# Steps between the stages of a two-layer decoder trunk: how norm sums, the last inner tile and the compressed keys reach the matrix engine

## The chip, the cores and the metric

The kernel runs on one core of one Trainium2 chip. The core has five engines, each with an instruction queue of its own that it works off in order: TensorE (PE in the profile; its weight loads are listed as PEld), VectorE (DVE), ScalarE (ACT), GpSimd (POOL) and SyncE (SP), which here issues the DMA transfers. The metric is the device time in microseconds (us) of one execution.

## The reference

One sequence of 256 tokens with 1024 channels goes through two layers. Each layer is a half-step SwiGLU FFN (inner width 2816), a mixer, and a second half-step FFN, each behind an RMS norm and added to the residual `h`:

```python
h = h + 0.5 * swiglu_ffn(rmsnorm(h, ffn1_norm[i]), ffn1_w_in[i], ffn1_w_out[i])
hn = rmsnorm(h, mix_norm[i])
if i < N_A_LAYERS:
    h = h + short_conv_mixer(hn, conv_w_in[i], conv_w[i], conv_w_out[i])
else:
    h = h + nsa_mixer(hn, attn_w_q[j], attn_q_norm[j], attn_w_o[j], rel_bias, kv)
h = h + 0.5 * swiglu_ffn(rmsnorm(h, ffn2_norm[i]), ffn2_w_in[i], ffn2_w_out[i])
```

Layer 1 mixes with a gated short convolution, layer 2 with an attention that has a compressed, a selected and a window branch. Between the layers one shared set of keys and values is made. The compressed keys are `rmsnorm(compress(...))`: blocks of 32 positions go through a two-layer perceptron (`gelu(blk @ w1) @ w2`, 64 output channels, 4 groups, 15 blocks), and the result is normed over the 64 channels. Everything is float32.

## The kernel before

**Products.** Activations lie transposed: channels on the 128 partitions, the 256 tokens along the free axis. A float32 operand is split into a high part (rounded to the type fp32r) and a low part (the rest). An activation tile holds both halves beside each other, 512 columns. For each 128x128 block of weights TensorE makes one product of 512 columns with the weight's high part `wh` (L315, L416) and one of 256 columns with its low part `wl` (L318, L418); the two halves in PSUM are added afterwards (`total`, L327 and L328). Plain float32 products are also used in a few places: TensorE runs each of them as two records.

**Weights.** `Stream` (L98) brings weights in pieces of 128x1024 ("units"): SyncE loads them (`ws`), ScalarE casts the high part (`high`, L148) and VectorE subtracts to get the low part (`low`, L165). There are six buffers for each half. `W.pump()` fills all that is free. The code's order is each engine's order: the kernel is written with a manual schedule, and a call to `W.pump()` puts its casts and subtractions into the queues of ScalarE and VectorE exactly there.

**Stages.** The first half of an FFN (`ffn_in`, L361) runs 22 tiles of two units; each tile's result is drained by `total`, multiplied with the norm's row factor `R`, gated (SiLU) and split into a hidden tile `hid` (`act` in the profile, L321 and L322). The second half (`out_proj`, L394) makes eight column tiles of the residual. For the FFNs each has 22 inner tiles: all high products, then all low ones (L416, L418). For the convolution's output product, with eight inner tiles, the first three column tiles are a "head": k = 0 to 6 of all three, and then k = 7 of each. After a column tile `out_evac` (L385) adds to `h` (L387, VectorE), prepares the next stage's operand `xs` (ScalarE L267, VectorE L271) and sums the squares on GpSimd into `sq` (L285, L286), with one unit's `low` and `high` between. `out_proj` ends with `W.pump()`; so does the attention's output product (L1142).

**The norm.** The next stage starts with `h` times the gain, unnormed; `R` is applied when a tile is drained. `Norm.rows` (L288) multiplies `sq` with a matrix of ones (one float32 product, L291), takes the root on ScalarE (L293) and the reciprocal on VectorE (L295). In the second FFN of each layer and in the convolution, this is done within the first tile: inner tiles 0 to 5, then 6, then `mid()` with the row sums, then 7.

**Tables and compressed keys.** `tables` loads the bias vector `rb` and a one-hot matrix, multiplies them (a float32 product with 33 rows, L250) in the first tile of layer 1's second FFN and writes the result to DRAM. The compressed keys are made in the background of layer 2's first FFN: `c_second` (L739, four groups of 16 columns), `kc_norm` on 16 partitions, `kc_trans` with two transposes.

## Time and profile before

| | |
|---|---|
| time, median of 3 runs | 978.57 us (978.12 to 978.57) |
| the profiled execution's own time | 978.35 us |
| its span, first to last instruction | 976.6 us |
| TensorE busy | 969.2 us (99%) |
| VectorE busy | 739.2 us (76%) |
| ScalarE busy | 559.8 us (57%) |
| GpSimd busy | 160.3 us (16%) |
| granted TensorE clock | 1.000 |

A row of the timeline reads: start, length, engine, line, operation, output <- inputs, shapes, count, and in brackets the idle time before it with what ended it. Rows that follow each other are merged. Matmul records overlap: the distance from start to start is what one costs.

### The profile page before, as it was taken

The numbers are of one execution on the slowest core, as the hardware profiler recorded it, in microseconds if no ns is written. First come the engines' busy times: TensorE is split into PE (matmuls) and PEld (weight loads), VectorE is DVE, ScalarE is ACT, GpSimd is POOL, SyncE is SP. The second block draws the span as 40 slices with busy tenths as digits, with TensorE's granted clock in tenths as the row PEclk, the third lists the DMA queues.
The fourth block names the chain that finished last, engine by engine and source line by source line (L and its number), as shares of the span: only waits on it lengthen the run. The fifth ranks groups of instructions, "written<-read, shape, count | busy, mean of one in ns | idle before, by whom it ended". The sixth has DMA issues, their size and how long they took to land. (4 is left out here: it accounts for less than half of the span.)

```text
span 976.6 us, 14680 instructions
## 1 busy us (share of the span) xinstructions
PE 969.2 (99%) x5680; PEld 845.9 (87%) x5680; DVE 739.2 (76%) x1175; ACT 559.8 (57%) x926; POOL 160.3 (16%) x249
## 2 busy tenths in 40 slices
PE   9999999999999999999999999999999999999998
PEld 7888888888888888888888888888887888888888
DVE  6988766668888778767549987866589898878652
ACT  6666553355556566644546677743489666656530
POOL 2000001144460000011111013001237330000000
PEclk9999999999999999999999999999999999999999
DMA  8565554546546775554635565655510356555550
GB/s 300 199 211 197 178 211 173 179 167 209 187 144 248 225 230 191 178 210 173 215 130 173 173 221 210 216 173 183 212 46 1 133 191 219 192 179 206 182 189 22
DMA packets 28289, 177.59 MB, mean 182 GB/s; under 512 B 3083, under 2 KB 6539, under 8 KB 7612
## 3 DMA queue, kind: packets, MB, share of 16 engines
q1 hardware_dynamic: 28220, 176.66, 53.1%
q8 instruction: 44, 0.72, 0.3%
q14 instruction: 25, 0.20, 0.1%
HBM read 175.57 MB, written 1.08 MB: 181 GB/s over the span
## 5 line engine op out<-in xcount | busy, mean ns | idle before, releaser
L165 DVE TENSOR_TENSOR wl<-ws,wh 128x1024 fp32r<-128x1024 f32 x320 | 393.9, 1245 | 97.9 <-PE a L418 60.1
L315 PE MATMUL mm<-xs,wh 128*128 128x512 f32 x1488 | 357.7, 392 | 0.0
L148 ACT CAST wh<-ws 128x1024 fp32r<-128x1024 f32 x320 | 331.5, 1047 | 40.4 <-PE a L416 21.7
L315 PEld LDWEIGHTS mm<-xs,wh 128*128 128x128 f32 x1488 | 273.2, 188 | 52.9
L318 PEld LDWEIGHTS mm<-xs,wl 128*128 128x128 f32 x1488 | 191.6, 191 | 7.8
L318 PE MATMUL mm<-xs,wl 128*128 128x256 f32 x1488 | 193.9, 283 | 0.0
L416 PE MATMUL a<-act,wh 128*128 128x512 f32 x722 | 171.6, 391 | 1.3 <-DVE act L322 1.3
L416 PEld LDWEIGHTS a<-act,wh 128*128 128x128 f32 x722 | 133.2, 188 | 29.1 <-DVE act L322 3.0
L328 DVE TENSOR_TENSOR t<-mm,t 128x512 f32<-128x512 f32 x96 | 66.1, 689 | 72.1 <-ACT t L327 71.5
L327 ACT COPY t<-mm 128x512 f32<-128x512 f32 x96 | 56.2, 586 | 98.3 <-PE mm L318 94.6
L418 PEld LDWEIGHTS a<-act,wl 128*128 128x128 f32 x722 | 91.4, 191 | 2.7
L418 PE MATMUL a<-act,wl 128*128 128x256 f32 x722 | 92.3, 283 | 0.0
L267 ACT ACTIVATE xs<-base 128x256 fp32r<-128x256 f32 x48 | 24.2, 508 | 91.8 <-DVE base L387 78.9
L343 ACT ACTIVATE t<-t 128x256 f32<-128x256 f32 x88 | 37.0, 420 | 62.9 <-DVE t L332 62.8
L332 DVE TENSOR_TENSOR t<-t,R 128x512 f32<-128x512 f32 x88 | 61.7, 701 | 2.9
L321 ACT CAST act<-t 128x256 fp32r<-128x256 f32 x96 | 39.1, 408 | 29.0 <-DVE t L533 19.1
L285 POOL TENSOR_TENSOR t<-base 128x256 f32<-128x256 f32 x35 | 27.2, 776 | 134.6 <-DVE base L387 133.0
L322 DVE TENSOR_TENSOR act<-t,act 128x256 fp32r<-128x256 f32 x96 | 41.0, 427 | 4.7 <-ACT act L321 4.7
L271 DVE SCALAR_TENSOR_TENSOR xs<-base,xs 128x256 fp32r<-128x256 f32 x48 | 30.2, 632 | 16.4 <-ACT xs L267 16.4
L282 POOL TENSOR_TENSOR sq<-base 128x256 f32<-128x256 f32 x5 | 3.1, 615 | 233.0 <-DVE base L387 224.8
L344 DVE TENSOR_TENSOR t<-t,t 128x256 f32<-128x256 f32 x88 | 37.0, 420 | 3.2 <-ACT t L343 3.0
L387 DVE SCALAR_TENSOR_TENSOR base<-a,base 128x256 f32<-128x256 f32 x78 | 32.9, 421 | 7.9 <-PE a L418 5.8
(246 smaller groups left out, 833.3 us busy)
## 6 DMA issues: line engine op xcount, KB each, us to landing
ws<-in_ffn_w_in_dram SPq DMA_DIRECT2D x85, 1024.0 KB, 5.0
ws<-in_ffn_w_out_dram SPq DMA_DIRECT2D x44, 1024.0 KB, 4.8
ws<-in_conv_w_in_dram SPq DMA_DIRECT2D x12, 1024.0 KB, 4.8
ws<-in_w_kv_dram SPq DMA_DIRECT2D x6, 1024.0 KB, 4.9
ws<-in_conv_w_out_dram SPq DMA_DIRECT2D x4, 1024.0 KB, 4.9
ws<-in_attn_w_q_dram SPq DMA_DIRECT2D x4, 1024.0 KB, 4.9
ws<-in_attn_w_o_dram SPq DMA_DIRECT2D x4, 1024.0 KB, 4.9
base<-row_d SPq DMA_DIRECT2D x8, 256.0 KB, 5.9
```

What stands on the lines that cost most here:

```text
L148: ac.copy(h, src)
L165: ve.tensor_tensor(out=l, in0=src, in1=h.bitcast(F32), op=ALU.subtract)
L315: pe.matmul(o, u[0][:, k * P:(k + 1) * P], xs[k], start=(k == 0), stop=False)
L318: pe.matmul(o[:, :T], u[1][:, k * P:(k + 1) * P], xs[k][:, :T], start=False, stop=(k == last))
L321: ac.copy(dst[:, :T], src)
L322: ve.tensor_tensor(out=dst[:, T:], in0=src, in1=dst[:, :T].bitcast(F32), op=ALU.subtract)
L327: ac.copy(r, o[:, :, T:])
L328: ve.tensor_tensor(out=r, in0=o[:, :, :T], in1=r, op=ALU.add)
L332: ve.tensor_tensor(out=r, in0=r, in1=R[:, None, :].to_broadcast([P, n, T]), op=ALU.mult)
L343: ac.activation(s, r[:, 0], AF.Silu)
L416: pe.matmul(o, wh, lhs[k], start=(k == 0), stop=False)
L418: pe.matmul(o[:, :T], wl, lhs[k][:, :T], start=False, stop=(k == n - 1))
```

## The change

Five edits:

1. `ones` is also read as fp32r, and `Norm.halves` splits `sq` into a high and a low half (`self.q`, ScalarE and VectorE); `sums` makes two fp32r products of 256 columns instead of one float32 product. `rows` takes these sums.
2. In the first tile of the convolution and of the second FFNs the row sums come after the whole tile, not inside it; the tile's `total` comes ahead of the root and the reciprocal.
3. In an FFN's `out_proj` the first column tile makes high and low products of k = 0 to 20 first, and then both of k = 21. In the convolution's, the head has four column tiles.
4. `tables` pads both operands to 128 partitions, splits the bias vector, casts the one-hot matrix on GpSimd and multiplies with two fp32r products after the first tile.
5. The compressed keys come out already transposed, from one product with the weights doubled to 128 columns; their squares are summed by a product with ones, and VectorE writes them into `KT`.

```diff
+        def halves(self):
+            self.q = act()
+            split(self.sq, self.q)
+
+        def rows(self, pb=None):
+
+            pb = pb or self.sums()
             s = t1()
...
+        def sums(self):
+            pb = bank()
+            for x in range(2):
+                pe.matmul(pb[:, :T], ones_r, self.q[:, x * T:(x + 1) * T], start=(x == 0), stop=(x == 1))
+            return pb
...
-        def mid():
+        if not n0 and R is None:
+            norm.halves()
             if pre is not None:
                 pre()
-            box[0] = norm.rows()
-
         for f in range(n0, NF):
             o = bank2()
             if f == n0 and n0:
                 box[0] = rms(o)
             else:
-                a_group([o[:, 0], o[:, 1]], xs, mid if f == 0 and R is None else None)
+                a_group([o[:, 0], o[:, 1]], xs, f == 0 and R is None)
+            if box[0] is None:
+                if pre is not None:
+                    pre()
+                pb = norm.sums()
             sums.append(total(o, 2))
+            if box[0] is None:
+                box[0] = norm.rows(pb)
...
-            head = [(bank(), W.take()[0]) for _ in range(3)]
+            head = [(bank(), W.take()[0]) for _ in range(4)]
             a_pass([(o, u, lhs, range(7)) for o, u in head])
...
+            for ks in (range(n - 1), [n - 1]) if c == 0 else (range(n),):
+                for k in ks:
+                    pe.matmul(o, run[k][0], lhs[k], start=(k == 0), stop=False)
+                for k in ks:
+                    pe.matmul(o[:, :T], run[k][1], lhs[k][:, :T], start=False, stop=(k == n - 1))
...
         yield
+        ohr, rbr = act(), act([P, 2, P])
+        po.tensor_copy(out=ohr, in_=oh)
+        ac.copy(rbr[:, 0], rb)
+        ve.tensor_tensor(out=rbr[:, 1], in0=rb, in1=rbr[:, 0].bitcast(F32), op=ALU.subtract)
+        yield
         pr = bank()
-        pe.matmul(pr[:16], rb, oh[:NB + 1], start=True, stop=True)
+        for x in range(2):
+            pe.matmul(pr, rbr[:, x], ohr, start=(x == 0), stop=(x == 1))
...
     def kv_mid():
         kv["rc"] = nm.cols()
+        nm.halves()
...
+    def kc_second(a):
+
+        d, pc = t1([P, 2, 64]), bank()
+        po.tensor_copy(out=d, in_=w2[0][:, None, :].to_broadcast([P, 2, 64]))
+        pe.matmul(pc[:, :64], d.rearrange("p a d -> p (a d)"), a, start=True, stop=True)
+        q = t1([P, 64])
+        ac.activation(q, pc[:, :64], AF.Square)
+        return pc, q
+
+    def kc_norm(pc, q):
+
+        pb = bank()
+        pe.matmul(pb[:, :64], ones, q, start=True, stop=True)
+        r = t1([P, 64])
+        ac.activation(r, pb[:, :64], AF.Sqrt, scale=1.0 / P, bias=epst)
+        ve.reciprocal(r, r)
```

The engines' orders at three places follow; numbers in names count buffers.

VectorE, from the last operand tile (`xs`) of the attention's output product into the first tile of layer 2's second FFN. Before:

```order
L271 SCALAR_TENSOR_TENSOR xs_7835<-base,xs_7835 128x256
L165 TENSOR_TENSOR wl_7985<-ws_7851,wh_7903 128x1024
L165 TENSOR_TENSOR wl_7987<-ws_7851,wh_7929 128x1024
L165 TENSOR_TENSOR wl_7991<-ws_7875,wh_7989 128x1024
L165 TENSOR_TENSOR wl_7997<-ws_7875,wh_7993 128x1024
L295 RECIPROCAL R_8032<-t_1402_8030 128x256
```

Now:

```order
L279 SCALAR_TENSOR_TENSOR xs_7848<-base,xs_7848 128x256
L165 TENSOR_TENSOR wl_7998<-ws_7864,wh_7916 128x1024
L165 TENSOR_TENSOR wl_8000<-ws_7864,wh_7942 128x1024
L165 TENSOR_TENSOR wl_8004<-ws_7888,wh_8002 128x1024
L165 TENSOR_TENSOR wl_8010<-ws_7888,wh_8006 128x1024
L339 TENSOR_TENSOR act_8012<-sq_7849,act_8012 128x256
L345 TENSOR_TENSOR t_1407_8051<-mm_8015,t_1407_8051 128x512
L306 RECIPROCAL R_8056<-t_1408_8054 128x256
```

The low half of the squares stands behind the four weight halves of `W.pump()`, and the drain of the first tile stands ahead of the reciprocal.

VectorE, at the same point of layer 1's second FFN (the residual and operand of the convolution's output product come first). Before:

```order
L165 TENSOR_TENSOR wl_2800<-ws_2660,wh_2731 128x1024
L271 SCALAR_TENSOR_TENSOR xs_2586<-base,xs_2586 128x256
L165 TENSOR_TENSOR wl_2811<-ws_2660,wh_2807 128x1024
L165 TENSOR_TENSOR wl_2815<-ws_2703,wh_2813 128x1024
L165 TENSOR_TENSOR wl_2821<-ws_2703,wh_2817 128x1024
L295 RECIPROCAL R_2863<-t_485_2861 128x256
```

Now:

```order
L165 TENSOR_TENSOR wl_2806<-ws_2681,wh_2737 128x1024
L279 SCALAR_TENSOR_TENSOR xs_2589<-base,xs_2589 128x256
L165 TENSOR_TENSOR wl_2817<-ws_2681,wh_2813 128x1024
L165 TENSOR_TENSOR wl_2821<-ws_2709,wh_2819 128x1024
L165 TENSOR_TENSOR wl_2827<-ws_2709,wh_2823 128x1024
L339 TENSOR_TENSOR act_2831<-sq_2590,act_2831 128x256
L254 TENSOR_TENSOR act_2835<-t_446_2592,act_2835 128x128
L345 TENSOR_TENSOR t_490_2881<-mm_2839,t_490_2881 128x512
```

Here the low halves of the squares and of the bias vector follow the three weight halves.

TensorE, in the first tile of the same stage. Before, the sums stand ahead of inner tile 7:

```order
L318 MATMUL mm_2825<-xs_2585,wl_2724 128x256
L250 MATMUL a_2854<-t_445_2591,rb 16x512
L291 MATMUL a_2859<-sq_2587,ones 128x256
L315 MATMUL mm_2825<-xs_2586,wh_2673 128x512
L315 MATMUL mm_2825<-xs_2586,wh_2701 128x512
L318 MATMUL mm_2825<-xs_2586,wl_2694 128x256
L318 MATMUL mm_2825<-xs_2586,wl_2724 128x256
```

Now:

```order
L332 MATMUL mm_2839<-xs_2589,wh_2694 128x512
L332 MATMUL mm_2839<-xs_2589,wh_2707 128x512
L335 MATMUL mm_2839<-xs_2589,wl_2700 128x256
L335 MATMUL mm_2839<-xs_2589,wl_2730 128x256
L258 MATMUL a_2872<-act_2834,act_2835 128x512 x2
L312 MATMUL a_2878<-act_2831,ones 128x256 x2
L332 MATMUL mm_2905<-xs_2582,wh_2737 128x512
```

The one-hot product and the sums have moved behind inner tile 7, in front of the second tile, and they read split operands.

## The prediction

> **What bounds the kernel now.** I read the page's shares of busy time first, then TensorE's timeline and its waits, and then the other engines' timelines around each change of stage.

> ```profile
> PE 969.2 (99%) x5680; PEld 845.9 (87%) x5680; DVE 739.2 (76%) x1175; ACT 559.8 (57%) x926; POOL 160.3 (16%) x249
> 32.13 3.82 PE L315 MATMUL mm<-xs,wh 128*128 128x512 f32 x16
> 35.78 2.08 PE L318 MATMUL mm<-xs,wl 128*128 128x256 f32 x16
> 37.69 3.82 PE L315 MATMUL mm<-xs,wh 128*128 128x512 f32 x16
> 133.15 0.69 DVE L328 TENSOR_TENSOR t<-mm,t 128x512 f32<-128x512 f32 x1 [1.17 <-ACT t L327]
> ```

> TensorE is busy 969.2 of 976.6 us, so nearly everything is paid for in TensorE's time: one product less saves its spacing, one stall costs its length. The spacing is read from starts: sixteen 512-column products take 35.78 - 32.13 = 3.65 us, 0.228 each; sixteen of 256 columns take 1.91, 0.120 each. A tile of an FFN's first half is 5.57 us. VectorE is idle for at least 1.17 us in such a tile (last row), so within a stage it catches up about a microsecond per tile. The question is what happens at the changes of stage, where VectorE is not idle.

> **The first column tile of the long output products (four places).** The change runs k = 0 to 20 of both weight halves before it touches the hidden tile that comes last.

> ```profile
> 132.33 4.95 PE L416 MATMUL a<-act,wh 128*128 128x512 f32 x21
> 137.13 0.42 DVE L322 TENSOR_TENSOR act<-t,act 128x256 fp32r<-128x256 f32 x1
> 137.60 0.50 PE L416 MATMUL a<-act,wh 128*128 128x512 f32 x1 [0.33 <-DVE act L322]
> 137.94 2.80 PE L418 MATMUL a<-act,wl 128*128 128x256 f32 x22
> PE a L416 <- DVE act L322: 1.3, 4, 0.3
> ```

> Twenty-one products at 0.228 end at 137.12, but the next starts at 137.60: 0.48 lost, and 0.11 more before the product after it (0.34 for 0.228). Now 21 x 0.120 = 2.52 us of low products come first, until 139.6, and the tile is there at 137.55. The whole 0.59 goes. TensorE's waits (the last row: 1.3 us in total, four times, 0.3 the longest) have the same step at all four places. **4 x -0.60 = -2.4 us.** No instruction is added.

> **The compressed keys.** Eight records of 16-column products, two transposes and a chain on 16 partitions become two small products over the whole array.

> ```profile
> 594.71 0.62 PE L742 MATMUL a<-small,t 128*16 128x64 f32 x8
> 595.26 3.96 PE L315 MATMUL mm<-xs,wh 128*128 128x512 f32 x16
> 600.98 0.56 PE L722 MATMUL a<-both,t 128*128 128x64 f32 x4
> 601.34 3.88 PE L315 MATMUL mm<-xs,wh 128*128 128x512 f32 x16
> 607.06 0.29 PE L775 MATMUL a<-small,t 16*128 16x16 f32 x2
> 607.28 3.94 PE L315 MATMUL mm<-xs,wh 128*128 128x512 f32 x16
> ```

> Removed: 0.55 + 0.22. Added: two fp32 products of 64 columns, two records each, of the kind of L722 (four in 0.36): 0.36 together. **-0.4 us** with the switches between shapes; a wait for the squares on ScalarE could halve it. One table load moves a tile later and stays under a tile's slack.

> **The norm's row sums as two fp32r products (four places).** At each, one fp32 product (two records) becomes two of 256 columns: 0.24 us.

> ```profile
> 197.13 1.23 DVE L165 TENSOR_TENSOR wl<-ws,wh 128x1024 fp32r<-128x1024 f32 x1 [0.46 <-ACT wh L148]
> 201.42 0.59 PE L291 MATMUL a<-sq,ones 128*128 128x256 f32 x2
> 788.34 2.91 PE L315 MATMUL mm<-xs,wh 128*128 128x512 f32 x12
> 790.56 0.81 POOL L286 TENSOR_TENSOR sq<-sq,t 128x256 f32<-128x256 f32 x1
> 790.69 5.17 DVE L165 TENSOR_TENSOR wl<-ws,wh 128x1024 fp32r<-128x1024 f32 x4
> 793.22 0.59 PE L291 MATMUL a<-sq,ones 128*128 128x256 f32 x2
> 794.36 2.89 PE L315 MATMUL mm<-xs,wh 128*128 128x512 f32 x12
> 795.78 1.74 DVE L295 RECIPROCAL R<-t 128x256 f32<-128x256 f32 x1
> 791.88 1.28 ACT L293 ACT_TABLE_LOAD   x1
> ```

> From 793.22 to 794.36 stand the sums and four products of k = 7 (2 x 0.228 + 2 x 0.120 = 0.70): the sums cost 0.44. The new form saves 0.20 at each place **if its operand is there**. That operand is new: a split of the squares, a copy on ScalarE and a subtraction on VectorE. For the convolution VectorE is done with its last weight half at 198.4, the subtraction is over by 198.8, and the sums now come at 202.3: **-0.2**. For the sums after the K/V products the split is issued a K/V matrix earlier, with as much room: **-0.2**.

> In the second FFN of layer 2 it is not there. Before, TensorE's sums read the squares as GpSimd leaves them, at 791.37. Now they also need VectorE's subtraction, and the order of VectorE puts it behind the four weight halves, which run from 790.69 to 795.86. It takes the reciprocal's place at 795.78 and, at L322's 0.42, ends at 796.20. TensorE ends its first tile at 788.34 + 5.57 = 793.91, does the high half's sums, and waits. The second tile starts at 796.25 + 0.12 = 796.4 against 794.36: **+2.0 us**. Behind this wait stands TensorE's whole next tile. The reciprocal, too, is later (sums, 1.28 of table load, the root), but the drain of PSUM ("total") now comes before it, and two tiles of weights are ready, 11 us of cover; without them it would cost up to 3 us.

> **Convolution's output product and the second FFN of layer 1.** Four column tiles instead of three run k = 0 to 6 first; the one-hot product becomes two fp32r products, and its operands have to be split as well.

> ```profile
> 261.30 4.95 PE L315 MATMUL a<-act,wh 128*128 128x512 f32 x21
> 268.68 0.43 DVE L322 TENSOR_TENSOR act<-t,act 128x256 fp32r<-128x256 f32 x1 [0.47 <-ACT act L321]
> 269.50 0.28 PE L318 MATMUL a<-act,wl 128*128 128x256 f32 x1
> 269.81 0.89 DVE L387 SCALAR_TENSOR_TENSOR base<-a,base 128x256 f32<-128x256 f32 x2 [0.71 <-PE a L318]
> 288.03 0.84 DVE L271 SCALAR_TENSOR_TENSOR xs<-base,xs 128x256 fp32r<-128x256 f32 x1
> 288.67 0.80 POOL L286 TENSOR_TENSOR sq<-sq,t 128x256 f32<-128x256 f32 x1
> 288.79 4.03 DVE L165 TENSOR_TENSOR wl<-ws,wh 128x1024 fp32r<-128x1024 f32 x3
> 289.24 1.03 PE L250 MATMUL a<-t,rb 33*16 33x512 f32 x2
> 289.41 0.53 POOL L559 MEMSET cbias<- 128x512 f32 x1
> 290.20 0.70 PE L291 MATMUL a<-sq,ones 128*128 128x256 f32 x2
> 291.44 3.80 PE L315 MATMUL mm<-xs,wh 128*128 128x512 f32 x16
> 292.75 1.74 DVE L295 RECIPROCAL R<-t 128x256 f32<-128x256 f32 x1
> ```

> On TensorE alone this is a gain. Three column tiles of seven steps and one high product more would bring the first tile's last low product to 261.30 + 21 x 0.228 + 21 x 0.120 + 0.228 = 268.84, but it started at 269.50: a stall of 0.66. The one-hot's 0.96 becomes 2 x 0.228, and the sums save 0.2: -1.4 in all. But the first column tile is now finished later. That low product started at 269.50; now it starts at 261.30 + 28 x 0.228 + 28 x 0.120 + 0.228 = 271.27. VectorE stands idle until it ends (the wait of 0.71 grows by 1.77), and from there to 292.75 VectorE waits for little but ScalarE's copies of its own results: it is VectorE, not TensorE, that sets the pace of the eight residual tiles. So everything on VectorE up to the last weight half is 1.77 later, 294.5 in place of 292.75. Then come the squares' subtraction (0.42, pitch 0.35) and that of the bias table, 128x128, which I bound by L758 and L322:

> ```profile
> 620.03 0.28 DVE L758 TENSOR_TENSOR vc<-a,t 32x128 fp32r<-32x128 f32 x1
> ```

> at 0.3. Both are done at 295.2. TensorE, through its products of k = 7 by 291.4 (they wait for xs at 288.87 + 1.77), waits for the second of these before the one-hot's second product: 295.2 + 0.23 + 0.24 = 295.65, against 291.44. **+4.2 us**, the three gains included. GpSimd's cast of the one-hot table starts at 289.94 + 1.77 = 291.7. The clear of the same size took 0.53 and a sum of half the size 0.80; between 0.5 and 3 us it is under VectorE's chain.

> **The sum.** -2.4 - 0.4 - 0.2 - 0.2 + 2.0 + 4.2 = **+3.0 us** against the profiled execution's 978.35 (span 976.6 and 1.75 around it): 981.3. That execution lies 0.2 under the median of the runs shown, so I say **981.5 us** beside 978.57. I call a difference under 0.2%, 2.0 us, no change that can be told here. Each VectorE term may be off by a queue position or by GpSimd's slowing (weight halves took 1.29 each at 790.69, 1.23 at 197.13): 0.3 per place, hence 980.5 to 982.6 for this case alone.

> **Rivals.**
> *The operands are in time.* If both splits came ahead of the weight halves, all six edits would be gains: -2.4 - 0.4 - 0.2 - 0.2 - 0.2 - 1.4 = -4.8, 973.8. For it: in layer 2 the squares are ready at 791.37, 2.5 us before the first tile ends (in layer 1, at 289.47, hardly). Against it: the order, in which no weight half stands behind the split. 9%.
> *Only part of the wait.* If the later first column did not reach the end of VectorE's queue (slack I overlooked between 271.3 and 292.75), the layer-1 place costs 1.8 less: +1.2, 979.8. If the layer-2 place does not wait, 2.2 less: +0.8, 979.4. 16%.
> *The stalls also slow the clock.* The kernel's start shows what an unused TensorE does:

> ```profile
> 1.05 3.78 PE L231 MATMUL a<-ones 128*128 128x128 f32 x16 [1.05 <-DVE ones L211]
> 0.00:5.00 5.00, 3.78 (x16) 3.49 (x16) 0.50 (x2) 2.36 (x5) 0.53 (x6) 1.00 0.57 161
> ```

> Sixteen passes of 128 columns in 3.78 us are over 0.21 each, what a pass of 256 columns takes at L291 (0.44 for two): half speed, although the granted clock of that window reads 1.00 (second row, third number from the end). If TensorE falls back so in the layer-1 stall and needs those 3.8 us again, it loses 1.9: 983.4. Against it: the 3.9 us there are broken by the k = 7 products and the one-hot's first, so no gap is over 2.5. 8%. [...]
> *The late reciprocal bites.* If the evacuation, 3 us late in three stages, does starve TensorE of weights, 0.5 to 1 each: 983 to 984. The 11 us of cover speak against it. 7%.

> **Numbers.** The forecast has 60%, the rivals 9, 16, 8 and 7. Range **979.3 to 983.4**: it leaves out the first rival and the ends of the others. Faster 9%. The partial case is mostly inside 0.2% (976.6 to 980.5), and the forecast's low end touches it: same 18%. Slower 73%.

> **What would show it.** Right: TensorE's products "a<-act,ones" idle for VectorE's "act<-sq" at two places, about 2.2 us in layer 2 and, with "a<-act,act" of the one-hot, 3 to 4 us in layer 1; no wait of the long output products for "act" in their first column tile; VectorE's first residual update of the convolution 1.8 us later relative to the first head product. Wrong: no such waits, or weight halves that stand behind the split; waits of TensorE for "wh" or "wl" inside a stage.

## The result, and the profile after

The changed kernel takes 985.9 us (median; 985.83 to 987.40) beside 978.37 for the kernel before on the same chip: a ratio of 1.0081, 95% interval 1.0068 to 1.0094. It is 7.5 us slower, where the prediction said 3.0 with a range up to 983.4. The profiled execution took 985.87 with a span of 984.1 (before: 978.35 and 976.6), and its mean granted clock is 0.995 where it was 1.000.

TensorE's share of busy time says nothing of this, since it is 99% in both. First the page's line, then TensorE's timeline of the changed kernel at the places of the prediction: start, length, line, operands, count, and in brackets the idle time ahead with what ended it.

```profile
PE 971.2 (99%) x5674; PEld 848.0 (86%) x5674; DVE 741.1 (75%) x1180; ACT 560.3 (57%) x930; POOL 161.0 (16%) x252
```

```profile
136.92 2.68 PE L436 MATMUL a<-act,wl 128*128 128x256 f32 x21
139.44 0.40 PE L434 MATMUL a<-act,wh 128*128 128x512 f32 x1
139.67 0.28 PE L436 MATMUL a<-act,wl 128*128 128x256 f32 x1
...
201.71 0.40 PE L312 MATMUL a<-act,ones 128*128 128x256 f32 x2
201.94 3.82 PE L332 MATMUL mm<-xs,wh 128*128 128x512 f32 x16
...
292.24 0.67 PE L258 MATMUL a<-act,act 128*128 128x512 f32 x1 [1.18 <-POOL act L252]
295.00 0.79 PE L258 MATMUL a<-act,act 128*128 128x512 f32 x1 [2.08 <-DVE act L254]
295.59 0.63 PE L312 MATMUL a<-act,ones 128*128 128x256 f32 x2
296.01 5.32 PE L332 MATMUL mm<-xs,wh 128*128 128x512 f32 x16
301.17 2.08 PE L335 MATMUL mm<-xs,wl 128*128 128x256 f32 x16
...
792.73 2.91 PE L332 MATMUL mm<-xs,wh 128*128 128x512 f32 x12
...
798.30 0.28 PE L312 MATMUL a<-act,ones 128*128 128x256 f32 x1
800.63 0.39 PE L312 MATMUL a<-act,ones 128*128 128x256 f32 x1 [2.05 <-DVE act L339]
800.85 5.41 PE L332 MATMUL mm<-xs,wh 128*128 128x512 f32 x16
806.10 2.08 PE L335 MATMUL mm<-xs,wl 128*128 128x256 f32 x16
```

To see where the time went, I took the start of the same tile in both timelines and followed their difference (after less before). It starts at -0.2, which is noise of the kernel's start.

| stage | difference goes from, to | change | forecast |
|---|---|---|---|
| first column tile of a long output product (each of four) | for instance -0.19 to -0.76 | -0.57 | -0.60 |
| convolution's sums | -0.76 to -0.97 | -0.2 | -0.2 |
| convolution's output product and second FFN, layer 1 | -0.97 to +6.09 | **+7.06** | +4.2 |
| sums after the K/V products | 5.52 to 5.31 | -0.2 | -0.2 |
| compressed keys | 5.31 to 4.97 | -0.34 | -0.4 |
| second FFN, layer 2 | 4.39 to 8.10 | **+3.71** | +2.0 |

All gains came as forecast: the stall in the first column tile is gone (no bracket from 136.92 to 139.67), and the sums take 0.23 (201.71 to 201.94). Both losses are where they were forecast, on the operands that were named, and both are too large.

Two rows show what was not forecast. The second tile of either FFN begins with sixteen products of 512 columns, 3.65 us from first start to the next group's in the kernel before. Now they take 301.17 - 296.01 = 5.16 and 806.10 - 800.85 = 5.25. TensorE waits for nothing there. The view by windows shows why; its columns are the window, its length, the busy time of each engine with the count of instructions (TensorE, its weight loads, VectorE, ScalarE, GpSimd), then the granted clock, and DMA's share and rate.

```profile
288.99:292.41 3.42, 1.70 (x9) 1.16 (x7) 3.42 (x4) 3.05 (x5) 3.12 (x4) 1.00 0.00 0
292.41:295.82 3.41, 1.33 (x4) 0.75 (x5) 2.53 (x4) 0.00 (x0) 0.00 (x0) 0.50 0.89 303
295.82:299.23 3.41, 3.41 (x10) 2.73 (x10) 2.32 (x2) 3.39 (x5) 0.00 (x0) 0.50 0.47 113
299.23:302.65 3.42, 3.42 (x22) 3.06 (x22) 3.39 (x6) 2.02 (x4) 0.00 (x0) 1.00 0.50 211
...
797.58:800.99 3.41, 1.36 (x9) 1.07 (x8) 3.41 (x5) 1.87 (x2) 0.00 (x0) 1.00 0.60 175
800.99:804.41 3.42, 3.42 (x10) 2.64 (x9) 3.00 (x4) 3.03 (x5) 0.00 (x0) 0.50 1.00 414
```

The clock is 0.50 for two windows of 3.41 us in layer 1 and for one in layer 2, and 1.00 elsewhere, as far as the span has records of it. The records begin at 5.69 us (at 6.36 in the trace before), and a stretch without records is printed as 1.00: that of the prediction's row from 0 to 5 us says nothing about the clock there. I set the edges of these windows by the records of the granted clock: it changes at 292.41, 299.23, 800.99 and 804.41, and 800.99 - 292.41 is 149 times 3.413. In the same way 299.23 - 292.41 = 6.82 is two such steps, 804.41 - 800.99 = 3.42 one. So in this trace the changes lie on a grid of steps of 3.413 us; the edges at which no change is recorded are reckoned from the others. In the window at half clock from 295.82 TensorE has 10 products where it has 22 in the next one, at full clock. In another execution the grid lies otherwise (an edge at 295.14, off this grid, in the run with three column tiles below).

VectorE's timeline in the two places, changed kernel:

```profile
270.99 0.88 DVE L404 SCALAR_TENSOR_TENSOR base<-a,base 128x256 f32<-128x256 f32 x2 [1.09 <-PE a L335]
...
289.96 4.44 DVE L165 TENSOR_TENSOR wl<-ws,wh 128x1024 fp32r<-128x1024 f32 x3
294.33 0.41 DVE L339 TENSOR_TENSOR act<-sq,act 128x256 fp32r<-128x256 f32 x1
294.66 0.28 DVE L254 TENSOR_TENSOR act<-t,act 128x128 fp32r<-128x128 f32 x1
...
795.07 5.17 DVE L165 TENSOR_TENSOR wl<-ws,wh 128x1024 fp32r<-128x1024 f32 x4
800.16 0.41 DVE L339 TENSOR_TENSOR act<-sq,act 128x256 fp32r<-128x256 f32 x1
```

The splits stand behind three and four weight halves, as the prediction had it. Layer 2's wait is its forecast: the second tile starts 6.49 later (800.85 against 794.36) where the first started 4.39 later, +2.1 for +2.0. Layer 1's second tile starts at 296.01 against 291.44, and TensorE came in 0.97 early: +5.5 for +4.2, of which 0.4 is already half clock (the second one-hot product and the sums, 1.01 where the kernel with both waits filled, below, takes 0.57 at full clock).

**Theories.** Theory 1: the order of VectorE makes TensorE wait, and a wait that empties enough of a grid window halves the clock of the next; together they are the whole loss beyond the gains. Its rivals: the half clock has another cause (the new products, the moment in the kernel); or the wait is not made by the split's place but by the four column tiles or by the convolution's later norm.

### The profile page after: what moved, and what is told of

It reads as the page before. It is cut to its first block, busy times and chain, and to the rows that moved or that the text cites. A ratio compares the mean times of both kernels' runs of the same rounds, so it can differ in the third digit from the quotient of the medians.

```text
span 984.1 us, 14668 instructions
## 1 busy us (share of the span) xinstructions
PE 971.2 (99%) x5674; PEld 848.0 (86%) x5674; DVE 741.1 (75%) x1180; ACT 560.3 (57%) x930; POOL 161.0 (16%) x252
## 4 chain that ended last, share of the span: by engine, by line
PE 84%; DVE 8%; ACT 4%; issue 2%; DMA 1%; POOL 1%; SPq 0%; DVEq 0%
PE mm L332 31%; PE mm L335 16%; PE a L434 16%; PE a L436 8%; DVE wl L165 3%; PE a L332 1%; ACT pr L996 1%; PE a L625 1%; PE a L627 1%; PE a L626 1%; ACT wh L148 1%; PE a L335 1%; DVE xs L279 1%; DMA base<-in_first_dram 1%; PE mm L503 1%
## 5 line engine op out<-in xcount | busy, mean ns | idle before, releaser
L165 DVE TENSOR_TENSOR wl<-ws,wh 128x1024 fp32r<-128x1024 f32 x320 | 393.9, 1245 | 93.7 <-PE a L436 65.0
L148 ACT CAST wh<-ws 128x1024 fp32r<-128x1024 f32 x320 | 330.9, 1045 | 40.4 <-PE a L434 21.8
L434 PE MATMUL a<-act,wh 128*128 128x512 f32 x714 | 169.2, 391 | 0.0
L293 POOL TENSOR_TENSOR t<-base 128x256 f32<-128x256 f32 x35 | 27.2, 777 | 135.8 <-DVE base L404 134.2
```

What stands on the lines that cost most here:

```text
L148: ac.copy(h, src)
L165: ve.tensor_tensor(out=l, in0=src, in1=h.bitcast(F32), op=ALU.subtract)
L434: pe.matmul(o, run[k][0], lhs[k], start=(k == 0), stop=False)
```

## The experiments

Each ratio is to the kernel before, run on the same chip beside the experiment; its median, 978.16 to 978.58, stands with each time that has a ratio.

### One part alone: the first column tile

```diff
 # kernel before, out_proj, products over 22 hidden tiles
-            for k, (wh, wl, end) in enumerate(run):
-                pe.matmul(o, wh, lhs[k], start=(k == 0), stop=False)
-            for k, (wh, wl, end) in enumerate(run):
+            for ks in (range(n - 1), [n - 1]) if c == 0 else (range(n),):
+                for k in ks: ...   # high half
+                for k in ks: ...   # low half
```

> The kernel before with one part of the change alone: in the first column tile of the four long output products, the last hidden tile is taken last. By the forecast's step, four stalls of 0.59 go: 2.4 us less than before, 976.0. The trace pair gives 0.57 per place, hence 2.3 less. Rival: the products are merely shifted and the stall returns at the tile's end; then 978.4, no change.

976.19 us beside 978.16, ratio 0.9978 (0.9969 to 0.9988): 2.0 less by the medians, 2.2 by the ratio. The waits of TensorE for the hidden tile (1.3 us, four times, before) are gone from its list. The term holds.

### The splits ahead of the weight halves

```diff
 # changed kernel
     out_proj(zs, 1.0, nm)                 # and the attention's output product
-        W.pump()                          # weight halves at its end
 def ffn_in(...):
     norm.halves(); pre()                  # splits
+    W.pump()                              # weight halves
```

> The changed kernel, but at the start of the two second FFNs the split of the squares (and, in layer 1, of the bias table) is issued ahead of the three or four weight halves instead of behind them. Theory 1 (VectorE's order makes TensorE wait, and the half clock follows from the wait): layer 2 loses its whole cost, 3.9 us (2.3 of wait, 1.6 of half clock); layer 1 loses most of its own, 4 to 6 us, since a wait of about 1 us for GpSimd's cast of the one-hot table and for the residual tiles stays; no half clock at either place; together 976 to 978. Theory 2 (the half clock has another cause, such as the heavier fp32r sums or where in time the place falls): the waits go but the two stretches at half clock stay, 3.6 us dearer: 980 to 982.

977.34 us beside 978.16, ratio 0.9992 (0.9982 to 1.0002): the whole loss of 7.5 us is gone, and the difference from the kernel before can't be told, by an exchange of neighbours on ScalarE's and VectorE's queues. The mean granted clock of the profiled execution is 1.000. TensorE's timeline:

```profile
291.81 0.98 PE L258 MATMUL a<-act,act 128*128 128x512 f32 x2 [0.63 <-POOL act L252]
292.62 0.40 PE L312 MATMUL a<-act,ones 128*128 128x256 f32 x2
292.86 3.80 PE L332 MATMUL mm<-xs,wh 128*128 128x512 f32 x16
...
793.59 0.40 PE L312 MATMUL a<-act,ones 128*128 128x256 f32 x2
793.82 3.82 PE L332 MATMUL mm<-xs,wh 128*128 128x512 f32 x16
```

In layer 2 nothing waits, and the stage is 0.2 us shorter than in the kernel before. In layer 1 2.2 us are left (the difference goes from -0.8 to +1.4). Theory 2 expected 980 to 982 and falls: the same products, without the wait, leave the clock alone.

### The wait filled with products, layer 2

```diff
 # changed kernel, ffn_in, layer 2
+    for x in range(18):
+        pe.matmul(fill[:, :T], ones_r, xs[0][:, :T], start=True, stop=True)
     pb = norm.sums()
```

> The changed kernel with 18 idle products of 256 columns (xs by ones, their sum is used by nobody) ahead of the row sums of layer 2's second FFN. They take 18 x 0.12 = 2.16 us, which is the length of TensorE's wait there, so the second row sum starts when it did. Theory 1 (a break of about 2.2 us in TensorE's work halves the clock for the next 3.4 us): the clock stays at 1.00 there and the second tile takes 3.8 instead of 5.4 us: 1.6 less than the changed kernel, 984.3. Theory 2 (half clock from another cause): no gain, 985.9 to 986.2.

985.50 us beside 978.16, ratio 1.0074 (1.0056 to 1.0092): the median lies less far below the changed kernel's than the 1.6 expected. The place itself did what was expected:

```profile
799.51 2.28 PE L395 MATMUL a<-xs,ones 128*128 128x256 f32 x18
801.63 0.60 PE L312 MATMUL a<-act,ones 128*128 128x256 f32 x2
802.06 3.81 PE L332 MATMUL mm<-xs,wh 128*128 128x512 f32 x16
```

From the last products of k = 7 to the third tile passed 8.11 us (799.51 to 807.62) in place of 9.71: 1.60 less, at clock 1.00. The rest of this execution was 1.2 us worse than the changed kernel's, 0.7 of it at the kernel's start and 0.5 in layer 1; why was not shown. So the total could not settle it; the next two runs could.

### Both waits filled

```diff
 # as above, and in layer 1, ahead of the one-hot products x = 0, 1
+    for y in range(9 + 7 * x):
+        pe.matmul(fill[:, :T], ones_r, xs[0][:, :T], start=True, stop=True)
     pe.matmul(pr, rbr[:, x], ohr, start=(x == 0), stop=(x == 1))
```

> The changed kernel with idle products of 256 columns in TensorE's waits of both second FFNs: 18 in layer 2, 9 and 16 ahead of the two one-hot products in layer 1. They lie inside the waits and end nothing later. Theory 1 (a window of 3.41 us in which TensorE stands for more than about 60% is followed by one at half clock): the clock is 1.000 in all executions, and the time is the changed kernel's less the 3.6 us that its half clock costs, 982.0 to 982.6. Rival (the clock does not follow TensorE's work): 985.5 to 986.

982.69 us beside 978.47, ratio 1.0043 (1.0028 to 1.0058), mean clock 0.999 to 1.000 in all four executions (in the trace it reads 1.00 around both filled waits, from 290.38 to 297.21 and from 795.19 to 802.01). In this trace layer 1's second FFN costs 5.1 and layer 2's 2.1, where the changed kernel's cost 7.06 and 3.71. So the half clock cost 1.9 + 1.6 = **3.5 us**, and the rest is waiting. Useless work in a wait made the kernel faster by more than 3 us.

### Which breaks halve the clock

```diff
 # kernel before, both FFNs without background work, after tiles 3, 5, ..., 21
+    pe.matmul(p[:, :T], ones, h[0], start=True, stop=True)
+    ac.copy(t, p[:, :T])
+    for _ in range(m):            # m = 1, 2, 3, 4, 5, 3, 4, 2, 6, 8
+        po.tensor_scalar(out=t, in0=t, scalar1=0.5, scalar2=None, op0=ALU.mult)
+    pe.matmul(q[:, :T], ones, t, start=True, stop=True)
```

> The kernel before with ten breaks put into TensorE's work in each of the two FFNs without background work: after every second tile two fp32 products of 256 columns with ScalarE's copy and 1 to 8 halvings on GpSimd between them (output as before, nobody reads the products). Each break lasts some 0.6 plus 0.3 to 0.5 a halving. Theory 1: a window of the 3.41 us grid of the granted clock in which TensorE stands for over about 60% (2.05 us) is followed by one at 0.5, one with under 53% is not; so breaks under 1.8 us never halve the clock, those of 2.1 to 3.4 us do or don't by where they fall in the grid. Rival (an idle time of 3.4 us in one piece is needed): only the longest breaks do. The whole costs some 50 us of breaks plus 1.7 us per halved window.

1141.3 us in its one execution; a halving on GpSimd took 0.85 where 0.3 to 0.5 was put down, so most breaks were far longer than planned, and only the shortest tell something. Three of them, TensorE's timeline:

```profile
167.15 0.70 PE L384 MATMUL a<-t,ones 128*128 128x256 f32 x2 [2.38 <-POOL t L383]
...
894.85 0.70 PE L384 MATMUL a<-t,ones 128*128 128x256 f32 x2 [1.46 <-POOL t L383]
...
909.44 1.04 PE L384 MATMUL a<-t,ones 128*128 128x256 f32 x2 [2.32 <-POOL t L383]
```

and the grid windows around them, each with the one behind it (edges reckoned in steps of 3.413 us from the changes of this run's clock):

```profile
162.14:165.56 3.42, 2.63 (x20) 2.19 (x18) 1.70 (x3) 1.21 (x4) 0.24 (x1) 1.00 0.32 72
165.56:168.97 3.41, 1.82 (x8) 1.56 (x9) 3.18 (x5) 2.74 (x5) 1.45 (x2) 1.00 0.56 235
168.97:172.39 3.42, 3.42 (x21) 2.99 (x20) 1.21 (x2) 0.13 (x1) 0.00 (x0) 1.00 0.48 134
...
892.60:896.01 3.41, 1.95 (x11) 1.41 (x10) 2.61 (x5) 1.93 (x4) 0.85 (x1) 1.00 0.65 195
896.01:899.43 3.42, 3.42 (x18) 2.85 (x18) 2.81 (x4) 1.65 (x3) 0.00 (x0) 1.00 0.41 168
906.25:909.66 3.41, 1.09 (x7) 0.69 (x6) 1.58 (x3) 1.95 (x4) 1.70 (x2) 1.00 0.80 269
909.66:913.08 3.42, 3.42 (x9) 2.69 (x9) 2.80 (x4) 1.61 (x3) 0.00 (x0) 0.50 0.09 38
```

Half clock follows the break of 2.32 us, and not the longer one of 2.38. The first lies in one window and leaves 1.09 us of busy TensorE in it; the second is cut by the grid and leaves 2.63 and 1.82. Six windows at full clock had at most 1.70 us of busy TensorE: two of the changed kernel (1.70 and 1.36), two of this run (1.09, and 1.20 from 49.50) and two of the run with three column tiles below (1.61 from 267.84, 1.41 from 291.73). Each was followed by one at 0.50. Four others, all of this run, were followed by full clock (1.82, 1.95, 2.63 and, from 46.09, 2.96), and one with 2.35 of another run was not (below). Of the windows at half clock, one with 1.33 us of busy TensorE was followed by another (292.41 of the changed kernel), and three with 3.41 or 3.42 by full clock (295.82 and 800.99 there, 35.85 here). The rival, that 3.4 us in one piece are needed, falls.

### The convolution's part alone

```diff
 # kernel before
+    nm.halves()                               # split of the squares
     for f in range(8):
         ...                                   # sums after the tile instead of inside it
 def conv_evac(f, ...):
+    pb = nm.sums() if f == 0 else None
     r = total(ocv, 2)                         # first drain
+    if f == 0: conv_norm(pb)                  # root, reciprocal
```

> The kernel before with the convolution's part alone: sums as two fp32r products, the norm's root and reciprocal behind the first drain of PSUM, three column tiles ahead as before. By the forecast's step (-0.2, nothing else): 978.0 beside 978.2. By the theory formed from the run with three tiles ahead (the convolution's results lag about 1.8 us to the end of the stage, TensorE waits 1.8 instead of 0.7 for the last of them and the next stage's chain on VectorE starts 1.8 later): 1.4 to 1.8 more than before, 979.6 to 980.0.

980.19 us beside 978.47, ratio 1.0023 (1.0012 to 1.0034): slower by 1.7, where the forecast's term was -0.2. TensorE's timeline of the output product:

```profile
266.50 2.67 PE L333 MATMUL a<-act,wl 128*128 128x256 f32 x21
270.97 0.50 PE L330 MATMUL a<-act,wh 128*128 128x512 f32 x1 [1.80 <-DVE act L337]
```

The wait for the last hidden tile is 1.80 instead of 0.40, because the convolution's results run later to the end of the stage. The lag starts in its first tile. The place of the root's table load on ScalarE, and of the reciprocal on VectorE, in the kernel before and then here:

```profile
197.12 1.28 ACT L293 ACT_TABLE_LOAD   x1
202.56 1.75 DVE L295 RECIPROCAL R<-t 128x256 f32<-128x256 f32 x1 [4.20 <-ACT t L293]
...
203.40 1.28 ACT L302 ACT_TABLE_LOAD   x1
205.19 1.75 DVE L304 RECIPROCAL R<-t 128x256 f32<-128x256 f32 x1 [1.09 <-ACT t L302]
```

Before, the load ran while ScalarE waited for the sums; now it stands behind the drain, and the reciprocal is 2.63 later. So is the first hidden tile of the stage, and the last still 1.81 (its split starts at 270.49 against 268.68). The three edits of this place were not tried singly. VectorE's first residual update comes 1.81 later (271.62 against 269.81), and layer 1's second FFN with it. Three of its eight executions took 981.4 to 981.9 at a mean clock of 0.998, the others 979.6 to 980.3 at 0.999 to 1.000: about one window at half clock that comes or not; what decides it was not shown, and the profiled execution is one without (980.11, mean clock 1.000).

### Three column tiles ahead, and four

```diff
 # first: changed kernel;  second: kernel before, with 3 -> 4
-            head = [(bank(), W.take()[0]) for _ in range(4)]
+            head = [(bank(), W.take()[0]) for _ in range(3)]
```

> The changed kernel with three column tiles ahead in the convolution's output product, as before, instead of four. Theory 1 (VectorE's chain from the first column tile to the last weight half sets the end of layer 1's change of stage, and four tiles ahead start it 1.8 to 2.1 later): 1.8 to 2.1 less than the changed kernel from the wait, and up to 1.7 more if one of the two windows at half clock goes: 982.1 to 984.1. Rival (the chain has slack, and the cost is the split behind the weight halves alone): the stall of 0.66 in the heads returns: 985.9 to 986.6.

983.45 us beside 978.16, ratio 1.0056 (1.0040 to 1.0072). The time is in the expected range and the reason is not. VectorE's first update came only 0.4 earlier relative to TensorE than with four tiles, not 1.8: with three, TensorE waits 1.80 for the last hidden tile, as in the run above. The four executions took 982.55, 982.89, 984.00 and 985.09 us at mean clocks of 1.000, 0.999, 0.997 and 0.995, where one window at half clock is 0.0017 of the mean: about none, none, two and three. Without half clock it is as fast as the changed kernel with its waits filled (982.69), so three or four tiles make little difference to the waits: layer 1's second tile comes 4.7 later in this trace, 5.1 with four tiles at full clock. What the median gained is mostly the clock, which halved less often; whether the place of the grid decides it (edges at 295.14 here, at 292.41 and 295.82 in the changed kernel) was not controlled. The number of windows alone does not give the price. One of the three in this trace, in the convolution's output product (271.25 to 274.67), cost nothing: VectorE's chain from the first update to the bias table's split took 23.96 with it and 23.95 in the changed kernel without. Two executions of the changed kernel itself at a mean clock of 0.997 took 985.88 and 985.93, as long as those at 0.995.

> The kernel before with one edit: four column tiles ahead instead of three in the convolution's output product. By the forecast's step, VectorE's first residual update comes 1.77 later and its chain sets the start of the next stage's second tile: 1.8 more, 980.2. Rival (the chain has slack, the heads' stall of 0.66 goes): 977.5 to 978.2.

979.85 us beside 978.58, ratio 1.0013 (1.0004 to 1.0023). VectorE's timeline (TensorE was 0.18 early there, which is to be added):

```profile
271.40 0.88 DVE L387 SCALAR_TENSOR_TENSOR base<-a,base 128x256 f32<-128x256 f32 x2 [2.48 <-PE a L318]
```

The first update is 271.40 - 269.81 + 0.18 = 1.77 later, exactly the forecast's figure. The second tile started 1.06 later, not 1.8: without the split TensorE waits for the residual tiles alone, and it gained the heads' stall of 0.66. So two parts of the change, each by itself, delay VectorE's chain by 1.8; together they delay it by 2.15, not 3.6, since four tiles ahead hide the convolution's lag. The forecast's 1.77 stood on one leg where there were two.

### The one-hot product as before

```diff
 # changed kernel, tables()
-    po.tensor_copy(out=ohr, in_=oh)           # cast, and split of the bias table
-    ...
-    for x in range(2): pe.matmul(pr, rbr[:, x], ohr, ...)
+    pe.matmul(pr[:16], rb, oh[:NB + 1], start=True, stop=True)
```

> The changed kernel with the one-hot product in fp32 as before: no cast of its table on GpSimd, no split of the bias table on ScalarE and VectorE. Theory 1 (the end of layer 1's wait is VectorE's split of the squares, and the bias table's split and the slower weight halves beside GpSimd's cast add 0.3 and 0.4 to it): 0.7 to 1.2 less from the wait, up to 1.7 less where a window at half clock goes: 983.5 to 985.5. Rival (the fp32r one-hot is a gain of 0.5): 986.4.

984.68 us beside 978.58, ratio 1.0065 (1.0050 to 1.0080); the interval overlaps the changed kernel's. In the trace, at the changed kernel's mean clock of 0.995, layer 1 costs 0.45 less. VectorE's timeline:

```profile
290.04 4.03 DVE L165 TENSOR_TENSOR wl<-ws,wh 128x1024 fp32r<-128x1024 f32 x3
294.00 0.41 DVE L333 TENSOR_TENSOR act<-sq,act 128x256 fp32r<-128x256 f32 x1
```

Without GpSimd's cast the three weight halves take 4.03 again, not 4.44. So the one-hot's fp32r form was no gain here. The one window in which the figures go the other way is here too, in the view by windows:

```profile
289.55:292.97 3.42, 2.35 (x8) 0.97 (x7) 3.42 (x4) 3.20 (x6) 1.56 (x3) 1.00 0.19 29
292.97:296.38 3.41, 1.92 (x5) 1.63 (x6) 2.83 (x4) 1.51 (x3) 0.00 (x0) 0.50 0.88 332
```

TensorE was busy for 2.35 us, and half clock followed. 1.03 us of it is the one-hot product on 33 rows and 16 columns of the array; whether that has to do with it was not tried and stays open.

### The gains without the losses

Kernel before with the first column tile, the compressed keys, the K/V sums, and layer 2's second FFN with the split first; then the same with layer 1's second FFN split first and the one-hot table loaded and split during the convolution:

```diff
+    tab = tables()
     for f in range(8):
+        if f in (1, 4): next(tab)             # load; cast and split
         ob, ocv = bank(), bank2()
```

> The kernel before with the parts of the change that gained: first column tile (-2.3), compressed keys (-0.35), sums after the K/V products (-0.2), and in layer 2's second FFN the split ahead of the weight halves (-0.25 in the run with the split first). Convolution and layer 1's second FFN as before. Theory 1 (the parts add): 975.1. Rival (they hide behind one another): 975.8 to 976.2, as the first column tile alone.

975.37 us beside 978.47, ratio 0.9969 (0.9957 to 0.9981). The interval alone does not exclude the rival; the trace does. Followed as above, TensorE's difference falls by 0.6 at each of the four column tiles, 0.15 at the K/V products, 0.34 at the compressed keys and 0.21 in layer 2's second FFN, 3.1 in all. The parts add.

> The same, and in layer 1's second FFN as well the split of the squares ahead of the weight halves, with the one-hot product as two fp32r products whose table is loaded and split during the convolution. Theory 1 (order and early operands make the fp32r form a gain there): 0.5 for the one-hot and 0.2 for the sums less, 974.4. Rival (VectorE's chain of residual tiles sets that place, so that TensorE's shorter work only waits longer): 975.1, no gain.

974.81 us beside 978.47, ratio 0.9963 (0.9950 to 0.9976). The intervals don't tell the two apart; TensorE's timeline does:

```profile
289.54 0.63 PE L258 MATMUL a<-act,act 128*128 128x512 f32 x2
290.00 0.48 PE L317 MATMUL a<-act,ones 128*128 128x256 f32 x2
290.33 3.81 PE L337 MATMUL mm<-xs,wh 128*128 128x512 f32 x16
```

Nothing waits, and the stage is 0.8 us shorter than in the kernel before (TensorE's difference goes from -0.32 to -1.11). This version beats both kernels.

## Why the prediction was wrong

The direction, both places and the operands were right. Of the 4.5 us by which the sum fell short:

- **Half clock behind the waits: 3.5 us.** The step that failed is the pricing of the two waits (+4.2 and +2.0): it counted the time in which TensorE stands, and took TensorE's own rate behind it as unchanged. The rival that named the clock had 8%, was priced in layer 1 alone (1.9; that layer 1 lost as much, 0.4 + 1.5, is luck, since the rival had TensorE run slow for 3.8 us and the trace has two windows, in the first of which it mostly stands), and was set low because no gap was over 2.5 us. The runs showed that no such gap is needed: half clock followed each of the six windows of 3.41 us in which TensorE was busy for 1.09 to 1.70 us. Layer 2's wait of 2.05 us falls into one window in the trace and left 1.36 us busy in it; there the prediction did not even ask.
- **Layer 1's wait: 5.1 instead of 4.2.** VectorE's chain started 2.15 later, not 1.77 (0.4); its weight halves took 4.44 beside GpSimd's cast, where 4.03 was assumed (0.4); the rest, 0.1, is within the reading. GpSimd's cast was called harmless between 0.5 and 3 us. TensorE did stand 1.18 for it, but VectorE's chain ended later still; the harm was in VectorE's three weight halves, 4.44 beside the cast and 4.03 in the run without it.
- **The convolution's sums: the term -0.2 is right for TensorE's sums and wrong for the edit.** Alone it costs 1.7. In the changed kernel the loss does not show as a term of its own, because the four tiles ahead hide most of it. The prediction counted the tiles as the cause and did not follow the later reciprocal to the end of the stage.

As forecast: -0.57 four times; compressed keys -0.34; K/V sums -0.2; layer 2's wait 2.1; the late reciprocal starved no tile (the tiles behind it in both second FFNs are 5.57). "Operands in time" is what the splits in front made of the kernel: 977.3, not 973.8, because the cast of the table (0.63) and VectorE's residual tiles (0.95 and 0.53) still hold up TensorE in layer 1.

## What to carry to other kernels

TensorE's stalls had two prices here: their length, and the half clock behind them, 1.6 us for the one window in layer 2 and 1.9 for the two in layer 1 (at most 1.7 for each by estimate, half of its 3.41 us, where TensorE sets the pace). Half clock followed each of the six windows that were left with 1.70 us or less of busy TensorE. Look for it in the granted clock around every new wait, not in the mean; and where a wait can't be taken away, products that nobody reads kept the clock up here at no cost that the trace shows (985.9 to 982.7 us). When an operand gets a new maker, ask what already stands ahead of it on the maker's queue: here two splits that stood behind three and four weight halves cost more than all other edits gained.
